# A blockwise inverse laid over 128 partitions instead of 64, even rows in one half and odd rows in the other

## The chip, the cores and the metric

One core of a Trainium2 chip runs the whole program. Its engines are PE (matrix products), DVE (vector), ACT (scalar functions), POOL (a second vector engine) and SP (here it issues every DMA). The metric is the device time of one execution in microseconds.

## The reference, cut to what matters

The program is one encoder layer: a normalised projection, an attention branch, and an RWKV-7 branch with 8 heads of 64 channels in two directions. The RWKV state follows this step, over 2048 and 512 tokens:

```python
def rwkv7_step(S, inp):
    r_t, w_t, k_t, v_t, kk_t, kka_t = inp
    s_kk = jnp.einsum('zbhvk,zbhk->zbhv', S, kk_t)
    S = S * w_t[..., None, :] - s_kk[..., :, None] * kka_t[..., None, :] + v_t[..., :, None] * k_t[..., None, :]
    return S, jnp.einsum('zbhvk,zbhk->zbhv', S, r_t)
```

The kernel computes it in chunks of 64 tokens. Within a chunk, the corrections `s_kk` of 64 tokens depend on one another through a triangular 64 x 64 matrix per head and direction, and the kernel inverts that matrix. It does so in blocks of 32: two triangular 32 x 32 blocks are inverted on DVE, and two small products on PE give the block that joins them.

## The kernel before, in words

The RWKV branch runs in 20 steps (`steps`): four pairs of heads, and in each of them five blocks of 512 tokens (one of them the short sequence) for the two directions. A step has two jobs (one per direction) of 8 chunks x 2 heads = 16 units, so 32 units of 64 x 64.

For each step, `prep` computes decays, the score matrices `SC` (L1177 masks them) and `AT` on PE, ACT, DVE and POOL. `inverse` then inverts, `chain_chunk` carries the state through 8 chunks per direction (its state update is L1289 on DVE, and the next chunk's first product L1259 on PE needs it), and `finish_job` normalises. Beside this, `feed` projects the next heads (L921) to keep PE filled. `do_chain(n)`, `do_inverse(n + 1)` and `do_prep(n + 2)` are written one behind the other, but this is not the order on the engines: every operation goes into a `Plan`, which lists them with a modelled cost and gives each engine a fixed order of its own by the longest remaining path. Each engine then executes its list in order. A tile lives in a named place in SBUF (`memory`, by `lay(tag, size, count)`); an operation that writes a tile whose place another tile used waits for that tile's last reader.

`inverse` in order:

- L1195: 8 DMAs per job bring the 32 x 32 diagonal blocks of `SC` to `ad` in DRAM, so that each of 64 blocks (32 units x 2) is one row of 1024 numbers. L1199 loads `ad` to `M`, 64 partitions x 32 x 32, in the lower half of the tile `X`.
- L1203 to L1206: the norms `ssd` give the scales `rm` and `rs`. L1209 scales the columns of `M`.
- The loop, L1213 and L1214, for i = 1 to 30: column i of `M` times row i, into `tmp`, and the sum into `M`. Both run on DVE on `i` rows and `31 - i` columns, 60 instructions per inverse, each needing the one before.
- L1215 sets the diagonal, L1216 scales the rows, L1217 (ACT) writes the transposed blocks to the upper half of `X`. L1219 stores the transposed blocks to `td[0]`, L1220 the others to `td[1]`.
- For each job: L1226 and L1227 load blocks back into `SC` (8 x 32 KB over the two jobs' units), L1230 loads the transposed first blocks into `bs`, 16 small products (L1233) go to PSUM, L1234 (ACT) copies them negated into `bs`, 16 more (L1237) follow, and L1242 copies the joined block into `SC`. The tile `bs` has one place, so the second job's L1230 waits for the first job's L1237.

## Time and profile before

| | |
|---|---|
| three runs, median (lowest to highest) | 2516.08 us (2509.64 to 2527.17) |
| the profiled execution | 2511.51 us, its span 2509.7 us |
| mean granted TensorE clock of that execution | 0.965 |
| PE, DVE, ACT, POOL busy | 2298.2, 1697.4, 1418.1, 870.8 us |

The span runs from the first to the last instruction of the profiled execution. Busy shares are averages over the span; where a wait matters is read in the stretch of the stage, from the chain of waits and from single rows in order of time. The profiler gives matmuls modelled ends, so PE at 93% of a stretch is not PE at its peak.

### The profile page before, as it was taken

What the parts mean: (1) busy time and instruction counts of PE and PEld (TensorE: products, weight loads), DVE (VectorE), ACT (ScalarE), POOL (GpSimd) and SP (SyncE); (2) the same over time, 40 slices, a digit from 0 to 9 for tenths busy, and PEclk for the clock granted to TensorE, in tenths of its full rate; (3) what the DMA queues carried; (4) which work ended last, traced back from release to release, by engine and by line L of the source; (5) the groups of instructions that cost most, each with busy time, mean ns of one, the idle gap of its engine ahead of it and who ended that gap; (6) DMA issues with size and microseconds to landing.
All of it is one profiled execution on the core that took longest, in us unless ns stands there. A gap on an engine that the chain in (4) does not pass through costs nothing.

```text
span 2509.7 us, 53916 instructions
## 1 busy us (share of the span) xinstructions
PE 2298.2 (92%) x20106; PEld 1652.1 (66%) x20106; DVE 1697.4 (68%) x4248; ACT 1418.1 (57%) x3264; POOL 870.8 (35%) x1059
## 2 busy tenths in 40 slices
PE   6999998987989998989999998999999899999996
PEld 5988997775654654656566665655665677767674
DVE  8874575165754566776887786777777886786445
ACT  7632343365665664667665667666667745554431
POOL 2472564001212154344444443444434533220100
PEclk9999999998999999999999999999999899999998
DMA  7343213367765765454544545655444565554546
GB/s 272 135 145 118 84 60 103 100 186 206 213 190 154 204 201 160 124 156 116 149 137 143 142 131 139 175 146 161 112 136 123 160 190 173 148 156 139 161 159 245
DMA packets 323639, 386.19 MB, mean 154 GB/s; under 512 B 132401, under 2 KB 197809, under 8 KB 321201
## 3 DMA queue, kind: packets, MB, share of 16 engines
q1 hardware_dynamic: 323376, 382.74, 51.9%
q8 instruction: 159, 2.61, 0.4%
q14 instruction: 104, 0.84, 0.1%
HBM read 261.36 MB, written 121.27 MB: 152 GB/s over the span
## 4 chain that ended last, share of the span: by engine, by line
PE 58%; DVE 15%; DMA 14%; ACT 8%; issue 4%; SPq 1%; POOL 1%; DVEq 0%; ACTq 0%; POOLq 0%
PE b L819 15%; PE b L921 11%; PE b L1393 6%; PE b L1175 5%; DVE sbuf L1213 3%; DVE sbuf L1214 3%; DVE sbuf L1289 3%; PE b L1259 3%; PE b L1269 2%; PE b L1262 2%; DMA sbuf<-vad 2%; PE b L1273 2%; PE b L1023 2%; DMA sbuf<-td 1%; DMA sbuf<-xd 1%
## 5 line engine op out<-in xcount | busy, mean ns | idle before, releaser
L921 PE MATMUL b<-sbuf 128*128 128x512 f16 x2040 | 562.6, 387 | 14.6 <-DMA sbuf<-xd 9.4
L819 PE MATMUL b<-sbuf 128*128 128x256 f16 x3840 | 458.5, 276 | 14.6 <-ACT sbuf L839 8.8
L819 PEld LDWEIGHTS <-sbuf 128*128 128x128 f16 x3840 | 374.9, 99 | 64.8 <-issue 12.5
L1393 PE MATMUL b<-sbuf 128*128 128x512 f32 x960 | 287.5, 428 | 20.6 <-DVE sbuf L1402 12.8
L921 PEld LDWEIGHTS <-sbuf 128*128 128x128 f16 x2040 | 177.9, 99 | 179.2 <-issue 22.8
L1289 DVE SCALAR_TENSOR_TENSOR sbuf<-b,sbuf 64x64 f32<-64x64 f32 x568 | 160.2, 282 | 163.9 <-ACT sbuf L1294 97.6
L1213 DVE TENSOR_TENSOR sbuf<-sbuf 64x30 f32<-64x30 f32 (+2 forms) x600 | 252.0, 420 | 11.2
L1214 DVE TENSOR_TENSOR sbuf<-sbuf 64x30 f32<-64x30 f32 (+2 forms) x600 | 247.9, 413 | 11.9
L1393 PEld LDWEIGHTS b<-sbuf 128*128 128x128 f32 x960 | 175.9, 196 | 66.6 <-DVE sbuf L1402 15.5
L1175 PE MATMUL b<-sbuf 128*128 128x128 f32 x1280 | 178.4, 288 | 2.8 <-DVE sbuf L1177 1.2
L1259 PE MATMUL b<-sbuf 128*128 128x128 f32 x608 | 140.8, 315 | 43.7 <-DVE sbuf L1289 25.6
L1175 PEld LDWEIGHTS b<-sbuf 128*128 128x128 f32 x1280 | 163.9, 200 | 16.4 <-issue 4.9
L1259 PEld LDWEIGHTS b<-sbuf 128*128 128x128 f32 x608 | 96.9, 194 | 111.3 <-DVE sbuf L1289 25.3
L1017 DVE CUSTOM_DVE_ANT_0 sbuf<-b,sbuf 128x384 f32<-128x384 f32 (+2 forms) x160 | 90.3, 580 | 113.0 <-PE b L1014 28.4
L1281 ACT ACTIVATE sbuf<-sbuf 128x128 f32<-128x128 f32 x284 | 113.1, 402 | 94.2 <-PE b L1259 91.7
L1273 PEld LDWEIGHTS b<-sbuf 128*64 128x64 f32 x1280 | 100.1, 137 | 85.0 <-ACT sbuf L1270 46.3
L1273 PE MATMUL b<-sbuf 128*64 128x64 f32 x1280 | 143.3, 235 | 13.8 <-ACT sbuf L1270 12.9
L1244 POOL MEMSET sbuf<- 64x512 f32 x80 | 41.1, 518 | 328.0 <-PE b L1277 197.4
L1277 PE MATMUL b<-sbuf 128*64 128x64 f32 x1280 | 152.4, 233 | 0.0
L1269 PE MATMUL b<-sbuf 128*64 128x64 f32 x1280 | 140.3, 235 | 10.0 <-ACT sbuf L1266 9.5
L1269 PEld LDWEIGHTS b<-sbuf 128*64 128x64 f32 x1280 | 100.2, 139 | 74.5 <-ACT sbuf L1266 42.5
L1294 ACT COPY sbuf<-b 64x128 f32<-64x128 f32 x320 | 83.6, 263 | 110.6 <-PE b L1277 57.5
(205 smaller groups left out, 4860.3 us busy)
## 6 DMA issues: line engine op xcount, KB each, us to landing
sbuf<-xd SPq DMA_DIRECT2D x60, 512.0 KB
sbuf<-zrk SPq DMA_DIRECT2D x80, 256.0 KB
sbuf<-zl SPq DMA_DIRECT2D x80, 256.0 KB
sbuf<-in_b_mid_dram SPq DMA_DIRECT2D x32, 512.0 KB
sbuf<-mix SPq DMA_DIRECT2D x28, 448.0 KB
sbuf<-in_x_dram SPq DMA_DIRECT2D x20, 512.0 KB
...
```

The source lines that it names most:

```text
L819: T.matmul(pa, xx[b][:, k, j * 128:(j + 1) * 128], wt[:, k], start=n == 0, stop=n == 23)
L921: T.matmul(pa, W[wt][:, k], xx[k], start=n == 0, stop=n == 23)
L1175: T.matmul(pa[:, u * 128:(u + 1) * 128], both(A[:, u]), z[:, u], start=True, stop=True)
L1213: V.tensor_tensor(out=prod, in0=bc(M[:, 0:i, i:i + 1], i, n), in1=bc(M[:, i:i + 1, i + 1:32], i, n), op=ALU.mult)
L1214: V.tensor_tensor(out=M[:, 0:i, i + 1:32], in0=M[:, 0:i, i + 1:32], in1=prod, op=ALU.add)
L1259: T.matmul(pz[:, 0:128], QR[:, c % 4].rearrange("p a s -> p (a s)"), S0, start=True, stop=False)
L1269: T.matmul(pu[0:64, l0:l0 + 64], SC[:, c % 4, h, 0:64], zs[:, l0:l0 + 64], start=True, stop=True)
L1273: T.matmul(pz[64:128, l0:l0 + 64], SC[:, c % 4, h, 64:128], UV[:, c % 4, l0:l0 + 64], start=S0 is None, stop=S0 is None or h == 1)
L1277: T.matmul(pu[l0:l0 + 64, 128:192], AT[:, c % 4, l0:l0 + 64], UV[:, c % 4, l0:l0 + 64], start=True, stop=True)
L1281: S.activation(out=S0, in_=S0, func=AF.Copy, scale=gt[:, gcol:gcol + 1])
L1289: V.scalar_tensor_tensor(out=S1[l, q], in0=src, scalar=by, in1=S0[l, q], op0=ALU.mult, op1=ALU.add)
L1393: T.matmul(pa, m, w, start=j == 0, stop=j == len(todo) - 1)
```

## The change

The 64 blocks now use 128 partitions. Partition u of the lower half holds the even rows of block u, partition 64 + u the odd rows, 16 rows of 32 each, in a tile `M` of its own. Since each step of the loop multiplies by row i of the block as it was loaded, both halves also get a whole copy of the block, `L` (in the place of `X`), which the loop reads and does not write. A step then runs over (i + 1)//2 rows instead of i.

`ad` is loaded by four DMAs, two whole (for `L`) and two with every second row (for `M`). The scales are prepared on 64 partitions as before, and three ACT copies spread them. The column scaling becomes two products. The transposing copy writes 512 numbers per partition into the front of `L`, with the rows in the order even, odd; the stores go to `tx` (transposed) and `tm` (two DMAs of every second row). `bs` is loaded by two DMAs per job, one per half, and the copy L1249 undoes the order of the columns. `tmp` has no place of its own any more: it is allocated in the one place of `bs`, and `M` takes the place where `tmp` was.

```diff
--- before.py
+++ after.py
@@ -579,7 +579,7 @@
     at = lay(at, *[(t, 32, 2) for t in ("wpam", "wpgs", "wsam", "wsgs", "sums")], ("m", 32, 4))
     end = lay(at, *[(t, 32, 2) for t in ("ss", "rsrx", "rstx", "waam", "wags", "hs")], ("wam", 32, 3),
               *[(t, 32, 1) for t in ("gm", "g8", "rsrg", "rstg")], *[(t, 64, 2) for t in ("ssq", "rsrn", "rstn")])
-    end = max(end, lay(at, ("rs", 256, 1), ("gt", 32, 6),
+    end = max(end, lay(at, ("rs", 384, 1), ("gt", 32, 6),
                        *[(t, 32, 2) for t in ("mean", "var", "rsrf", "rstf")]))
     K = end
     X = K + 40 * KB
@@ -606,7 +606,7 @@
     lay(A, ("lw0", 2 * KB, 1), ("lw1", 2 * KB, 1), ("uph0", KB, 1), ("upl0", KB, 1), ("uph1", KB, 1), ("upl1", KB, 1),
         ("rt", 2 * KB, 2), ("kt", 2 * KB, 2), ("smt", 2080, 1), ("s2", 2080, 1), ("Em", 2080, 1), ("E", 2080, 1),
         ("tha", 2 * KB, 1), ("AK", 2 * KB, 2), ("mkt", KB, 1), ("st", 512, 2), ("rkb", 512, 2),
-        ("QR", 2 * KB, 5), ("bs", 2 * KB, 1), ("tmp", KB, 1), ("zs0", 512, 2), ("zs1", 512, 2))
+        ("QR", 2 * KB, 5), ("bs", 2 * KB, 1), ("M", 2 * KB, 1), ("zs0", 512, 2), ("zs1", 512, 2))
     lay(A + 50 * KB, ("wrh", 2 * KB, 2), ("wrl", 2 * KB, 2), ("AT", 2 * KB, 1), ("QR", 2 * KB, 1))
     lay(end, ("fy", 2 * KB, 1))
     lay(X, ("xx", 4 * KB, 4), ("wrh", 2 * KB, 2), ("wrl", 2 * KB, 2), ("UV", 2 * KB, 6), ("yt", 2 * KB, 3),
@@ -1193,45 +1193,61 @@
                 for k in range(2):
                     l0 = 32 * k
                     D.dma_start(dst[k][:, 8 * i:8 * i + 8], units(SC[l0:l0 + 32])[:, :, l0:l0 + 32])
-        X = tile([128, 32, 32], F32, tag="X", name="X")
-
-        M, X = X[0:64], X[64:128]
-        D.dma_start(M.rearrange("p s t -> p (s t)"), ad)
-        rs = tile([64, 2, 32], F32, tag="rs", name="rs")
-        rm, rs = rs[:, 0], rs[:, 1]
+
+
+        L = tile([128, 32, 32], F32, tag="X", name="L")
+        M = tile([128, 16, 32], F32, tag="M", name="M")
+        rows = lambda ap: ap.rearrange("u (a q t) -> q u a t", q=2, t=32)
+        half = (slice(0, 64), slice(64, 128))
+        for q, l in enumerate(half):
+            D.dma_start(L[l].rearrange("p s t -> p (s t)"), ad)
+            D.dma_start(M[l], rows(ad)[q])
+        rs = tile([128, 3, 32], F32, tag="rs", name="rs")
         for d, J in enumerate(jobs):
-            D.dma_start(rm[32 * d:32 * d + 32], ssd[p][J["b"]][d].rearrange("c h (k t) -> (c h k) t", t=32))
-        V.tensor_scalar(out=rm, in0=rm, scalar1=1e-24, scalar2=2.0, op0=ALU.max, op1=ALU.mult)
-        V.reciprocal(rs, rm)
-        V.tensor_scalar(out=rm, in0=rs, scalar1=-1.0, scalar2=None, op0=ALU.mult)
-        tmp = tile([64, 256], F32, tag="tmp", name="tmp")
-        bc = lambda ap, n, m: ap.to_broadcast([64, n, m])
-        V.tensor_tensor(out=M, in0=M, in1=bc(rm[:, None, :], 32, 32), op=ALU.mult)
+            D.dma_start(rs[32 * d:32 * d + 32, 0], ssd[p][J["b"]][d].rearrange("c h (k t) -> (c h k) t", t=32))
+        V.tensor_scalar(out=rs[0:64, 0], in0=rs[0:64, 0], scalar1=1e-24, scalar2=2.0, op0=ALU.max, op1=ALU.mult)
+        V.reciprocal(rs[0:64, 1], rs[0:64, 0])
+        V.tensor_scalar(out=rs[0:64, 0], in0=rs[0:64, 1], scalar1=-1.0, scalar2=None, op0=ALU.mult)
+        S.copy(out=rs[64:128, 0], in_=rs[0:64, 0])
+        for q, l in enumerate(half):
+            S.copy(out=rs[l, 2, 0:16], in_=rs[0:64, 1, q::2])
+        rm, rs = rs[:, 0], rs[:, 2, 0:16]
+        tmp = tile([128, 256], F32, tag="bs", name="tmp")
+        bc = lambda ap, n, m: ap.to_broadcast([128, n, m])
+        V.tensor_tensor(out=M, in0=M, in1=bc(rm[:, None, :], 16, 32), op=ALU.mult)
+        V.tensor_tensor(out=L, in0=L, in1=bc(rm[:, None, :], 32, 32), op=ALU.mult)
         for i in range(1, 31):
-            n = 31 - i
-            prod = tmp[:, 0:n * i].rearrange("p (s t) -> p s t", t=n)
-            V.tensor_tensor(out=prod, in0=bc(M[:, 0:i, i:i + 1], i, n), in1=bc(M[:, i:i + 1, i + 1:32], i, n), op=ALU.mult)
-            V.tensor_tensor(out=M[:, 0:i, i + 1:32], in0=M[:, 0:i, i + 1:32], in1=prod, op=ALU.add)
-        G.memset(M.rearrange("p s t -> p (s t)")[:, 0:1024:33], 1.0)
-        V.tensor_tensor(out=M, in0=M, in1=bc(rs[:, :, None], 32, 32), op=ALU.mult)
-        S.copy(out=X.rearrange("p t s -> p s t"), in_=M)
-        td = dr.tile([2, 64, 1024], F32, tag="td", name="td", bufs=2)
-        D.dma_start(td[0], X.rearrange("p s t -> p (s t)"))
-        D.dma_start(td[1], M.rearrange("p s t -> p (s t)"))
+
+            n, r = 31 - i, (i + 1) // 2
+            prod = tmp[:, 0:n * r].rearrange("p (s t) -> p s t", t=n)
+            V.tensor_tensor(out=prod, in0=bc(M[:, 0:r, i:i + 1], r, n), in1=bc(L[:, i:i + 1, i + 1:32], r, n), op=ALU.mult)
+            V.tensor_tensor(out=M[:, 0:r, i + 1:32], in0=M[:, 0:r, i + 1:32], in1=prod, op=ALU.add)
+        for q, l in enumerate(half):
+            G.memset(M[l].rearrange("p s t -> p (s t)")[:, q:512:34], 1.0)
+        V.tensor_tensor(out=M, in0=M, in1=bc(rs[:, :, None], 16, 32), op=ALU.mult)
+        X = L[:].rearrange("p s t -> p (s t)")[:, 0:512]
+        S.copy(out=X.rearrange("p (t a) -> p a t", a=16), in_=M)
+        tm = dr.tile([64, 1024], F32, tag="tm", name="tm", bufs=2)
+        tx = dr.tile([128, 512], F32, tag="tx", name="tx", bufs=2)
+        D.dma_start(tx, X)
+        for q, l in enumerate(half):
+            D.dma_start(rows(tm)[q], M[l])
         for d, J in enumerate(jobs):
-            t_ = td[0, 32 * d:32 * d + 32].rearrange("(u k) (s t) -> k s u t", k=2, t=32)
-            tt = td[1, 32 * d:32 * d + 32].rearrange("(u k) (s t) -> k s u t", k=2, t=32)
+            tt = tm[32 * d:32 * d + 32].rearrange("(u k) (s t) -> k s u t", k=2, t=32)
             SU = {i: units(SC[:]) for i, SC in J["SC"].items()}
             for i, t in SU.items():
                 D.dma_start(t[0:32, :, 0:32], tt[0][:, 8 * i:8 * i + 8])
                 D.dma_start(t[32:64, :, 32:64], tt[1][:, 8 * i:8 * i + 8])
             bs = tile([64, 16, 32], F32, tag="bs", name="bs")
             t11 = bs[0:32]
-            D.dma_start(t11, t_[0])
+            for q in range(2):
+                D.dma_start(t11[:, :, 16 * q:16 * q + 16],
+                            tx[64 * q + 32 * d:64 * q + 32 * d + 32].rearrange("(u k) (t a) -> k t u a", k=2, a=16)[0])
             pb = bank("inv")
             for u in range(16):
                 T.matmul(pb[32:64, 32 * u:32 * u + 32], SU[u // 8][0:32, u % 8, 32:64], t11[:, u], start=True, stop=True)
-            S.activation(out=bs[32:64].rearrange("p u t -> p (u t)"), in_=pb[32:64], func=AF.Copy, scale=-1.0)
+            S.activation(out=bs[32:64].rearrange("p u (a q) -> p u a q", q=2),
+                         in_=pb[32:64].rearrange("p (u q a) -> p u a q", q=2, a=16), func=AF.Copy, scale=-1.0)
             pb = bank("inv")
             for u in range(16):
                 T.matmul(pb[0:32, 32 * u:32 * u + 32], bs[32:64, u], SU[u // 8][32:64, u % 8, 32:64],
```

On DVE, this is the place where the eleventh inverse's loop begins, before the change. L1289 is the chain's state update, L691 to L693 and L1154 belong to `finish_job` and `prep`, L1209 scales `M`, and L1213 and L1214 are the loop's first pair.

```order
L1289 SCALAR_TENSOR_TENSOR sbuf<-b_18324,sbuf 64x64 x2
L692 TENSOR_TENSOR sbuf<-sbuf 128x8
L693 SCALAR_TENSOR_TENSOR sbuf<-sbuf 128x8
L691 SCALAR_TENSOR_TENSOR sbuf<-sbuf 128x8
L692 TENSOR_TENSOR sbuf<-sbuf 128x8
L1209 TENSOR_TENSOR sbuf<-sbuf 64x1024
L1154 SCALAR_TENSOR_TENSOR sbuf<-sbuf 128x4x64
L1213 TENSOR_TENSOR sbuf<-sbuf 64x30
L1154 SCALAR_TENSOR_TENSOR sbuf<-sbuf 128x4x64
L1214 TENSOR_TENSOR sbuf<-sbuf 64x30
```

After the change, the same place of the same inverse (L1217 scales `M`, L1223 and L1224 are the loop's first pair, and L1305 is the chain's state update, L1289 before):

```order
L1217 TENSOR_TENSOR sbuf<-sbuf 128x512
L1305 SCALAR_TENSOR_TENSOR sbuf<-b_18520,sbuf 64x64 x2
L692 TENSOR_TENSOR sbuf<-sbuf 128x8
L1154 SCALAR_TENSOR_TENSOR sbuf<-sbuf 128x4x64
L693 SCALAR_TENSOR_TENSOR sbuf<-sbuf 128x8
L1154 SCALAR_TENSOR_TENSOR sbuf<-sbuf 128x4x64
L1305 SCALAR_TENSOR_TENSOR sbuf<-b_18658,sbuf 64x64 x2
L1223 TENSOR_TENSOR sbuf<-sbuf 128x30
L1224 TENSOR_TENSOR sbuf<-sbuf 128x30
L1223 TENSOR_TENSOR sbuf<-sbuf 128x29
```

The loop's first pair has moved back: between the tenth inverse's closing product and it stand 42 instructions now and 25 before, among them 13 of the chain's updates where there were 5. Between the tenth loop's first and last instruction stand 30 others now and 43 before; over all twenty loops, 762 now and 950 before. In 15 of the twenty inverses the first L1223 carries a wait on PE.

On SP, at the same inverse, this is the return of the tenth inverse's blocks before the change (L1226, L1227 and L1230 load from `td`, L1199 loads the eleventh's blocks, L965, L1119 and L1245 are other stages):

```order
L1227 DMA sbuf<-td 32x8x32
L1230 DMA sbuf<-td 32x16x32
L1199 DMA sbuf<-ad 64x1024
L1227 DMA sbuf<-td 32x8x32
L1226 DMA sbuf<-td 32x8x32
L1227 DMA sbuf<-td 32x8x32 x2
L1226 DMA sbuf<-td 32x8x32
L965 DMA zrk_3_18163<-sbuf 128x512
L1119 DMA sbuf<-zl_8430 128x512
```

The second job's L1230 stands 15 rows behind the first. After the change (L1239 and L1240 load from `tm`, L1244 from `tx` into `bs`, L1203 and L1204 the eleventh's blocks):

```order
L1244 DMA sbuf<-tx 32x16x16 x2
L1240 DMA sbuf<-tm 32x8x32 x2
L1195 DMA ad<-sbuf 32x8x32 x2
L1240 DMA sbuf<-tm 32x8x32 x2
L1239 DMA sbuf<-tm 32x8x32 x2
L1203 DMA sbuf<-ad 64x1024 x2
L1204 DMA sbuf<-ad 64x16x32 x2
L1119 DMA sbuf<-zl_8430 128x512
L1244 DMA sbuf<-tx 32x16x16 x2
L1239 DMA sbuf<-tm 32x8x32
```

All loads of the eleventh's blocks now stand between the first job's pair L1244 and the second's, and the second pair has moved up: it stands eight rows behind the first.

## Rows read from the trace of the kernel before

**Rows 1.** Page, part 1: engine, busy us (share of the span), instructions

```profile
PE 2298.2 (92%) x20106; PEld 1652.1 (66%) x20106; DVE 1697.4 (68%) x4248; ACT 1418.1 (57%) x3264; POOL 870.8 (35%) x1059
```

**Rows 2.** Stretch 930 to 2320: length, busy by engine, granted clock, DMA share, GB/s

```profile
930.00:2320.00 1390.00, 1293.91 (x11432) 877.02 (x11431) 1060.50 (x2576) 872.87 (x2079) 550.89 (x752) 0.97 0.52 146
```

**Rows 3.** Chain that ended last, 930 to 2320, shares by line

```profile
by line: PE b L921 12.6%; PE b L1175 7.8%; DVE sbuf L1213 5.3%; PE b L1393 5.2%; DVE sbuf L1214 5.1%; issue 4.5%; DVE sbuf L1289 4.5%; PE b L1259 4.1%; PE b L1269 3.4%; PE b L1262 3.4%; PE b L1273 2.7%; DMA sbuf<-td 2.3%; DMA sbuf<-xd 2.2%;
```

**Rows 4.** Page, part 5, the loop: shapes, count | busy, mean ns | idle before

```profile
L1213 DVE TENSOR_TENSOR sbuf<-sbuf 64x30 f32<-64x30 f32 (+2 forms) x600 | 252.0, 420 | 11.2
L1214 DVE TENSOR_TENSOR sbuf<-sbuf 64x30 f32<-64x30 f32 (+2 forms) x600 | 247.9, 413 | 11.9
```

**Rows 5.** Single lines: count, ns min/median/max, first and last start

```profile
L1213 DVE TENSOR_TENSOR sbuf<-sbuf x600: 170/370/1390, 932.5 to 2314.4; 64x30 f32<-64x30 f32 x10, 64x130 f32<-64x130 f32 x10, 64x198 f32<-64x198 f32 x10, 64x234 f32<-64x234 f32 x10
L1209 DVE TENSOR_TENSOR sbuf<-sbuf x20: 1208/1218/1698, 930.8 to 2281.6; 64x1024 f32<-64x1024 f32 x20
L1217 ACT COPY sbuf<-sbuf x20: 1909/1974/2119, 985.7 to 2316.2; 64x1024 f32<-64x1024 f32 x20
L1234 ACT ACTIVATE sbuf<-b x40: 589/589/592, 996.7 to 2336.5; 32x512 f32<-32x512 f32 x40
```

**Rows 6.** Timelines of DVE, POOL: start, us, line, shapes [idle before]

```profile
1669.12 0.18 DVE L1213 TENSOR_TENSOR sbuf<-sbuf 64x30 f32<-64x30 f32 x1
...
1698.35 0.40 DVE L1213 TENSOR_TENSOR sbuf<-sbuf 64x240 f32<-64x240 f32 x1
...
1578.87 1.27 POOL L1316 TENSOR_TENSOR sbuf<-sbuf 128x512 f32<-128x512 f32 x1 [0.45 <-ACT sbuf L1294]
1579.17 2.05 DVE L1216 TENSOR_TENSOR sbuf<-sbuf 64x1024 f32<-64x1024 f32 x1
```

**Rows 7.** DVE by shape, whole span: busy us, mean ns | idle before

```profile
L1209 DVE TENSOR_TENSOR sbuf<-sbuf 64x1024 f32<-64x1024 f32 x20 | 26.5, 1325 | 42.2 <-DMA sbuf<-ad 42.1
L848 DVE TENSOR_TENSOR sbuf<-sbuf 128x1024 f32<-128x1024 f32 x20 | 25.5, 1273 | 0.7
```

**Rows 8.** Waits, 930 to 2320: who waited for what, us, times, longest

```profile
DVE sbuf L1209 <- DMA sbuf<-ad: 42.1, 17, 5.0
PE b L1259 <- DVE sbuf L1289: 24.0, 53, 1.3
```

**Rows 9.** Timelines of DVE and PE from the tenth to the eleventh inverse

```profile
1526.47 0.35 DVE L1213 TENSOR_TENSOR sbuf<-sbuf 64x30 f32<-64x30 f32 x1
...
1593.08 0.17 DVE L1213 TENSOR_TENSOR sbuf<-sbuf 64x30 f32<-64x30 f32 x1
...
1604.38 1.19 PE L1237 MATMUL b<-sbuf 32*32 32x32 f32 x32
```

**Rows 10.** Timeline of SP's DMA issues at the same place

```profile
1586.56 0.44 SPq L1230 DMA_DIRECT2D sbuf<-td  x1
1587.09 0.47 SPq L1199 DMA_DIRECT2D sbuf<-ad  x1
...
1595.54 0.43 SPq L1230 DMA_DIRECT2D sbuf<-td  x1
```

**Rows 11.** ACT by shape, 1300 to 2000

```profile
L1172 ACT COPY sbuf<-sbuf 64x512 f32<-64x512 f32 x78 | 48.0, 616 | 18.1 <-PE b L1175 11.7 <-POOL sbuf L1163 2.2 <-POOL sbuf L1160 1.9
L1294 ACT COPY sbuf<-b 64x128 f32<-64x128 f32 x159 | 41.6, 263 | 44.0 <-PE b L1277 19.2 <-DVE sbuf L1289 17.1 <-PE b L1262 4.1
```

**Rows 12.** DMA, 1176.5 to 1178.5: packets, MB; the queue's share of 16 engines

```profile
DMA packets 1546, 0.20 MB, mean 100 GB/s; under 512 B 1540, under 2 KB 1540, under 8 KB 1546
q1 hardware_dynamic: 1546, 0.20, 60.6%
```

**Rows 13.** Longest pieces of the chain: start, us; L1217 alone, first and last of nine

```profile
1107.12 1.95 ACT sbuf L1217
...
2160.40 2.08 ACT sbuf L1217
```

## The prediction

> **What bounds the kernel now.** I read the busy shares first. PE is busy 92% of the span, DVE 68%, ACT 57%, POOL 35% [rows 1]. The change touches one stage only, the twenty calls of `inverse`, which run from 930 to 2320 us, so I read that stretch next: of its 1390 us PE is busy 1293.9, DVE 1060.5, ACT 872.9, and the 16 DMA engines 0.52 [rows 2]. PE is therefore the fullest engine and only 96 us of the stretch are left without a matmul; no relief elsewhere can give back more than that. The view to weigh a DVE change by is the chain of waits of the same stretch: the two lines of the inverse's loop, L1213 and L1214, hold 5.3% and 5.1% of it, 144.6 us, and loads from `td` 2.3%, 32 us [rows 3]. Their busy time is 252.0 + 247.9 = 499.9 us in 1200 instructions, 25.0 us per inverse [rows 4]. So 29% of the loop's busy time sets the end and 71% lies beside PE's work.
>
> Then I followed one inverse into the next, the tenth into the eleventh. The tenth's first product starts at 1526.47, its closing product L1216 at 1579.17 [rows 6, 9]. The eleventh's first product starts at 1593.08, while the tenth's last group of small matmuls (L1237) runs until 1604.38 + 1.19 = 1605.57 [rows 9]. The inverses thus overlap by 12.5 us: one iterates on DVE while the other's blocks still come back through DRAM, PE and ACT.
>
> **The change part by part.**
>
> *The loop.* Its 60 instructions stay; each covers half the rows. Undisturbed, 30 elements took 0.18 us and 240 took 0.40 [rows 6]: 1.05 ns per element and 0.149 us fixed. Before, each of the two lines streams the sum of i(31-i) = 4960 elements per partition; after, the sum of (31-i) times (i+1)//2 = 2600. An inverse saves 2 x 2360 x 1.05 ns = 4.95 us; undisturbed it goes from 8.9 + 10.4 = 19.3 to 14.4. That twice the partitions cost nothing is read from 1024 elements on 64 partitions (1325 ns) and on 128 (1273) [rows 7]. The measured 25.0 is 5.7 over the undisturbed 19.3, with single products up to 1390 ns [rows 4, 5]. Do these 5.7 shrink too? One row shows what they are: POOL ran L1316 from 1578.87 to 1580.14, and L1216, begun at 1579.17, took 2.05 us [rows 6], which is the rest of POOL's instruction plus about the 1.1 to 1.2 us of its own. The delay is the remainder of a POOL instruction and not a share of the DVE one, so I let all 5.7 stand: 25.0 becomes 20.05, minus 19.8%. (The Trainium skill, "SBUF — State Buffer", section "Who interferes with whom", says that a DVE instruction with two SBUF inputs and a GpSimd instruction that reads SBUF exclude each other for a whole instruction, with no sharing. By that rule, as by the row, the loss per inverse stays at 5.7; were bandwidth shared instead, the saving would be 25.0 x 4.95 / 19.3 = 6.4 us and the term below 37 us instead of 28.6.) On the chain: 144.6 x 0.198 = **-28.6 us**.
>
> *Closing.* L1216 goes from 1024 to 512 elements, -0.54 us. The transposing copy L1217 takes 1.97 us [rows 5]; half as many elements at its own rate is 0.98 (between 0.62, what 512 plain elements took on ACT [rows 11], and 1.97 if only partitions were added). Among the longest pieces of the chain the copy stands whole nine times, from 1107 to 2160 us [rows 13]. So 9 x (0.54 + 0.98) = **-13.7 us**.
>
> *The return.* The t11 block is loaded by two DMAs of 512 pieces of 64 bytes for one of 512 pieces of 128. One more issue is 0.44 us [rows 10]. Pieces: in two microseconds that held almost only small ones, 1546 took 60.6% of 16 engines, 12.5 ns each [rows 12]; 512 more are 0.4 us over 16 engines. The two t11 loads of an inverse are in series (one `bs` slot): +1.7 us. L1234 takes 0.59 us [rows 5] and now reads and writes with strides; bounds are no loss and a doubling (L1217's 1.93 ns an element against 1.2 for a plain 512), and I take +0.3, twice. Together +2.3 us per inverse, on the chain in the same nine: **+20.7 us**.
>
> *The loads.* `ad` is read by four DMAs instead of one (3 x 0.47 us of SP [rows 10]), 2048 of their pieces 128 bytes; `rs` passes through three small ACT copies (0.26 us each by the nearest row [rows 11]); L1209 becomes two products of 0.68 and 1.22 us. Today DVE waits 42.1 us for that load, 17 times [rows 8], so it would cost: about 3 us of loading, 0.8 of copies and 0.7 of product. I cost it at **nothing** because of the next part: the loop cannot begin earlier anyway. Without that cover it is 20 x 4.5 = 90 us on DVE's queue, of which the loop's 29% is 26 on the chain.
>
> *The new wait.* `tmp` now lies in the slot of `bs`, so the loop's first product must wait until the previous inverse's last L1237 has read `bs`. In the order, 15 of the 20 first products carry a wait on PE. At the handover that moves the loop from 1593.08 to 1605.57 or later, 12.5 us. Behind that product on DVE's in-order queue stand the chain's L1289, for which PE waits (24.0 us in the stretch [rows 8]). The order answers by putting other work ahead of it: 42 instructions instead of 25 between closing product and first product at this handover, and 762 instead of 950 others inside the twenty loops. Is there room? A cycle is (2281.6 - 930.8)/19 = 71.1 us [rows 5]. The tenth inverse's loop lasted 52.7 us with 43 others inside. One that is not the loop's takes (1060.5 - 499.9)/(2576 - 1200) = 0.41 us [rows 2, 4], so 25.0 + 17.6 were work and 10.1 gaps. After, with 30 inside: 20.05 + 12.3 + 10.1 = 42.5. The return lasted 1605.57 - 1579.17 = 26.4 and becomes 26.4 + 0.8 = 27.2. In series 69.7 us, which is under 71.1: I take **0**, with 1.4 us of room.
>
> *Off the path.* 5184 more pieces per inverse (2048 loading, 1984 + 64 storing, 64 for the second copy of L, 1024 for t11) at 12.5 ns are 4.1 us of 16 engines, 81 us in all: 0.52 becomes 0.58. (The Trainium skill, "DMA: Bandwidth & Descriptors", section "Specifications", speaks against such pieces: under 512 bytes an engine reads, modifies and writes. The rows agree that they are poor, about 10 GB/s an engine, but hold too few stores to show a doubling. By that rule, taken as a doubling, the 2048 pieces stored into `tm` cost 1.6 us more per inverse; that store runs beside the copy L1229, so the sum stays.)
>
> **Sum.** -28.6 - 13.7 + 20.7 = -21.6 us. The profiled execution took 2511.5 us (span 2509.7), 4.6 under the median of the three runs; 2511.5 - 21.6 = 2489.9, so I say **2490 us**.
>
> **The rivals.**
>
> *PE takes it all back.* PE is at 93%; where DVE comes sooner, another PE row may stand first. For it: PE's matmuls hold most of the chain. Against it: 96 us without a matmul. Result within 8 us of 2511.
>
> *More than the chain shows.* With 99 us less on DVE the L1289 rows queue less, and half of PE's 96 idle us close: 2511.5 - 48 = 2463. For it: DVE carries 42.5 - 10.1 = 32.4 us in a loop window instead of 42.6. Against it: those L1289 waits are partly for ACT, which hardly changes.
>
> *The new wait becomes the loop that sets the pace (slower).* Place: L1223 behind the last L1253 of the inverse before. It decides from the point where loop and return together pass 71.1 us, 1.4 us away. What could use that up: on SP the second pair of t11 loads now stands eight rows behind the first (before, fifteen), so SP halts there until the first job's L1253; before, L1230 was issued at 1586.56 and 1595.54 [rows 10], 9 us apart, with useful loads between. If 3 us per cycle are lost so, 1.6 remain over the room: 19 x 1.6 = 30 us, and nothing of the gain is left: 2542.
>
> That the wider products don't run faster per row is excluded by [rows 7].
>
> **How the numbers follow.** Forecast (gain of 5 to 50 us): 0.45. PE takes it back: 0.20. More than the chain shows: 0.14. The new wait sets the pace: 0.21. One per cent, 25 us, is about what a measurement of this kernel can tell from no change. Half of the forecast's cases lie beyond 25 us, as do all of the third's: faster 0.36. Of the last, three quarters lie beyond +25: slower 0.16. Same: 0.48. The range runs from inside the third case to the last case's price, 2445 to 2542; the forecast's own is 2462 to 2506.
>
> **What would show it.** DVE's loop lines at about 400 us (from 499.9), means near 335 ns: right. If under 370, the POOL delays shrank too. L1217's successor near 0.98 us, L1234's at 0.6 to 1.2. DVE waits of the first L1223 for PE: short ones mean room; several us in most handovers, with PE below 93% in the stretch, mean that the rival holds and the time is above 2511. A DMA share over 0.62 would say that the pieces cost more than 12.5 ns. The forecast is wrong if the loop lines fall as said and the stretch does not shorten.

## The result, and the profile after

The changed kernel takes **2547.11 us** (median of 4; 2544.39 to 2559.95) against 2513.76 us for the kernel before on the same chip (4; 2509.64 to 2527.17). The ratio is **1.0161** (95%: 1.0128 to 1.0194). The two medians alone give 1.0133, 33 us; 1.61% would be 40 us, and the interval holds both. The forecast was 2490 us, with 2445 to 2542 as its range: the time lies 57 us above the forecast and 5 above the range, on the other side of no change.

The profiled execution after has a span of 2543.3 us at a granted clock of 0.954; before it was 2509.7 at 0.965. Its page, the engines first (busy us, share of the span, instructions), then the DMA packets, then the loop's two lines (count | busy us, mean ns of one | idle before):

```profile
PE 2316.7 (91%) x20106; PEld 1664.7 (65%) x20106; DVE 1609.2 (63%) x4268; ACT 1403.2 (55%) x3324; POOL 853.2 (34%) x1079
...
DMA packets 429241, 396.71 MB, mean 156 GB/s; under 512 B 236720, under 2 KB 302128, under 8 KB 426800
...
L1223 DVE TENSOR_TENSOR sbuf<-sbuf 128x30 f32<-128x30 f32 (+2 forms) x600 | 200.1, 334 | 18.1 <-PE b L1253 5.8
L1224 DVE TENSOR_TENSOR sbuf<-sbuf 128x30 f32<-128x30 f32 (+2 forms) x600 | 192.2, 320 | 12.3
```

DVE lost 88 us of work [rows 1] and the loop 107.6: 499.9 us [rows 4] became 392.3. What the change is for, it does. And yet PE is busy 18 us longer with the same 20106 matmuls.

The chain that ended last, 930 to 2350 us, shares by line:

```profile
by line: PE b L921 9.7%; PE b L1409 6.3%; PE b L1175 5.9%; issue 4.9%; DVE sbuf L1223 4.1%; DVE sbuf L1305 3.9%; DVE sbuf L1224 3.2%; PE b L1275 3.2%; PE b L1285 3.0%; PE b L1278 2.9%; PE b L1289 2.3%; PE b L1248 1.9%; PE b L1253 1.9%; ACT 
```

Against [rows 3] the loop's share falls from 10.4% to 7.3%, from 144.6 to 103.7 us. So 41 us did leave the chain, and something else filled the place.

Now the stretch in which all the loss lies, 920 to 2600 us (length, busy time of PE, weight loads, DVE, ACT and POOL, then granted clock, DMA share, GB/s), before and after. The stretch runs past the end of the shorter span, so idle PE time is span less 920 less busy time:

```profile
920.00:2600.00 1680.00, 1466.63 (x12548) 996.30 (x12546) 1155.05 (x2792) 935.59 (x2243) 572.15 (x775) 0.97 0.49 144
```

```profile
920.00:2600.00 1680.00, 1487.44 (x12566) 1010.55 (x12564) 1068.36 (x2816) 923.58 (x2305) 556.12 (x795) 0.95 0.55 150
```

Before, 1589.7 us were left, 1466.6 of them busy: 123.1 idle. After, 1623.3 and 1487.4: 135.9 idle. Of the 33.6 us by which the profiled span grew, 12.8 are idle PE time and **20.8 are more busy time for the same matmuls**, in a stretch with a granted clock of 0.95 instead of 0.97 (means over time spent at 2.4 and at 1.2 GHz). The mean clock does not settle the busy time by itself: **own_tmp**, a run below, has nearly the idle time (2525.0 - 920 - 1469.6 = 135.4 us) and the clock (0.956) of after, and its PE is busy only 2.9 us longer than before. So how much of the 20.8 the clock makes stays open. The stretch of own_tmp:

```profile
920.00:2600.00 1680.00, 1469.56 (x12535) 1012.77 (x12533) 1086.19 (x2809) 919.15 (x2298) 565.42 (x792) 0.95 0.54 150
```

Over many runs, clock and time do go together. Over the 86 executions of the kernel before that stand beside the runs below (2491.64 us at 0.972 to 2523.96 at 0.963), a fitted line gives 17 us per 0.01 of clock. The 0.011 between the two profiled executions are worth 19 us by it. That says what goes with what, and not which causes which. The next rows show one place in which the clock falls behind idle time.

After, at 1206.92 us, the chain waits 6.21 us for a load of `xd`, the operand of L921, from its issue to its landing. First the chain's piece (start, us, what), then five stretches around it in the columns above, then the packets under way while PE waits:

```profile
1206.92 6.21 DMA sbuf<-xd
```

```profile
1186.00:1189.90 3.90, 3.63 (x37) 2.02 (x35) 2.21 (x5) 2.94 (x8) 1.97 (x5) 1.00 0.51 114
1189.90:1197.20 7.30, 7.26 (x53) 5.06 (x51) 5.69 (x13) 6.67 (x17) 0.00 (x1) 1.00 0.82 203
1197.20:1206.90 9.70, 7.99 (x111) 6.16 (x111) 3.16 (x6) 8.11 (x19) 6.73 (x12) 1.00 0.84 161
1206.90:1213.20 6.30, 4.80 (x73) 3.85 (x73) 2.83 (x7) 2.89 (x8) 1.49 (x2) 0.94 0.94 262
1213.20:1223.00 9.80, 9.66 (x83) 5.56 (x82) 5.07 (x16) 3.78 (x11) 2.78 (x6) 0.87 0.83 283
```

```profile
DMA packets 2455, 1.65 MB, mean 262 GB/s; under 512 B 1795, under 2 KB 2027, under 8 KB 2454
## 3 DMA queue, kind: packets, MB, share of 16 engines
q1 hardware_dynamic: 2454, 1.64, 93.8%
```

The DMA engines are full (0.94), 1795 of 2455 packets are under 512 bytes, PE drops from 7.26 of 7.30 us to 7.99 of 9.70 and then 4.80 of 6.30, and the clock from 1.00 to 0.87 in the stretch after. The averages of the stage (0.57 DMA, 0.95 clock) show none of this. It is one place; how much such places cost in all is what the runs with whole pieces below measure.

### The profile page after: what moved, and what is told of

Its sections match the earlier page's. It is cut to its first block, busy times and chain, and to the rows that moved or that the text cites. A ratio compares the mean times of both kernels' runs of the same rounds, so it can differ in the third digit from the quotient of the medians.

```text
span 2543.3 us, 54276 instructions
## 1 busy us (share of the span) xinstructions
PE 2316.7 (91%) x20106; PEld 1664.7 (65%) x20106; DVE 1609.2 (63%) x4268; ACT 1403.2 (55%) x3324; POOL 853.2 (34%) x1079
## 4 chain that ended last, share of the span: by engine, by line
PE 27%; DVE 11%; ACT 5%; DMA 5%; issue 3%; SPq 2%; POOL 1%; DVEq 0%; ACTq 0%; POOLq 0%
PE b L1409 7%; PE b L921 5%; PE b L1175 3%; DVE sbuf L1305 2%; DVE sbuf L1223 2%; PE b L1275 2%; PE b L1285 2%; DVE sbuf L1224 2%; PE b L1278 2%; PE b L1289 1%; PE b L1248 1%; ACT sbuf L1310 1%; PE b L1253 1%; DMA sbuf<-tx 1%; DMA sbuf<-xd 1%
## 5 line engine op out<-in xcount | busy, mean ns | idle before, releaser
L921 PE MATMUL b<-sbuf 128*128 128x512 f16 x2040 | 571.0, 391 | 20.9 <-DMA sbuf<-xd 16.8
L921 PEld LDWEIGHTS <-sbuf 128*128 128x128 f16 x2040 | 179.5, 99 | 193.1 <-issue 37.6
L1305 DVE SCALAR_TENSOR_TENSOR sbuf<-b,sbuf 64x64 f32<-64x64 f32 x568 | 160.5, 283 | 175.9 <-ACT sbuf L1310 86.2
L1223 DVE TENSOR_TENSOR sbuf<-sbuf 128x30 f32<-128x30 f32 (+2 forms) x600 | 200.1, 334 | 18.1 <-PE b L1253 5.8
L1224 DVE TENSOR_TENSOR sbuf<-sbuf 128x30 f32<-128x30 f32 (+2 forms) x600 | 192.2, 320 | 12.3
L1293 PE MATMUL b<-sbuf 128*64 128x64 f32 x1280 | 157.9, 236 | 0.0
L1289 PEld LDWEIGHTS b<-sbuf 128*64 128x64 f32 x1280 | 101.7, 140 | 85.1 <-ACT sbuf L1286 48.5
L1289 PE MATMUL b<-sbuf 128*64 128x64 f32 x1280 | 144.5, 237 | 11.1 <-ACT sbuf L1286 10.1
L1177 DVE TENSOR_TENSOR sbuf<-b,sbuf 128x512 f32<-128x512 f32 x160 | 109.9, 689 | 62.5 <-PE b L1175 38.2
L1278 PE MATMUL b<-sbuf 128*64 128x64 f32 x1280 | 146.0, 237 | 1.4 <-DMA sbuf<-tm 0.8
L1285 PE MATMUL b<-sbuf 128*64 128x64 f32 x1280 | 140.7, 236 | 6.9 <-ACT sbuf L1282 6.1
```

Source lines behind the costliest of these rows:

```text
L921: T.matmul(pa, W[wt][:, k], xx[k], start=n == 0, stop=n == 23)
L1223: V.tensor_tensor(out=prod, in0=bc(M[:, 0:r, i:i + 1], r, n), in1=bc(L[:, i:i + 1, i + 1:32], r, n), op=ALU.mult)
L1224: V.tensor_tensor(out=M[:, 0:r, i + 1:32], in0=M[:, 0:r, i + 1:32], in1=prod, op=ALU.add)
L1278: T.matmul(pz[0:64, l0:l0 + 64], SC[:, c % 4, h, 0:64], UV[:, c % 4, l0:l0 + 64], start=S0 is None, stop=S0 is None or h == 1)
L1285: T.matmul(pu[0:64, l0:l0 + 64], SC[:, c % 4, h, 0:64], zs[:, l0:l0 + 64], start=True, stop=True)
L1289: T.matmul(pz[64:128, l0:l0 + 64], SC[:, c % 4, h, 64:128], UV[:, c % 4, l0:l0 + 64], start=S0 is None, stop=S0 is None or h == 1)
```

## Experiments: the relief by itself

**before_half** is the kernel before with the loop over (i + 1)//2 rows on its 64 partitions: the shorter instructions alone.

```diff
-            n = 31 - i
-            prod = tmp[:, 0:n * i].rearrange("p (s t) -> p s t", t=n)
+            n, r = 31 - i, (i + 1) // 2
+            prod = tmp[:, 0:n * r].rearrange("p (s t) -> p s t", t=n)
```

> The kernel before with the loop over (i + 1)//2 rows instead of i, still on 64 partitions: the products and sums of the other rows are left out. It has the relief of DVE (about 99 us busy) and nothing else of the change: no second load, no copies, no new wait, no other return. The prediction's term by the chain of waits: 28.6 us faster, 2480 to 2490. The rival that PE takes it all back: within 8 us of before. The rival that the chain of waits undervalues it: below 2470.

Measured: 0.9992 (0.9973 to 1.0012). The loop is as short as it should be (400.3 us busy) and nothing is gained. But the plan models each instruction's cost, so a shorter loop also gives a new order on every engine. **half_fixed** leaves the instructions of before_half and charges the plan the old cost, so that the order on every engine is that of before:

```diff
-        op = Op(len(self.ops), eng, call, args, kw, self.cost(eng, call, out, reads, kw), self.boost)
+        op = Op(len(self.ops), eng, call, args, kw, self.cost(eng, call, out, reads, kw) if self.full is None else 0.068 + self.full * 0.00104, self.boost)
...
+            plan.full = n * i
```

> As before_half (loop over (i + 1)//2 rows on 64 partitions; the other rows' products are left out), but the planner still counts the full rows, so that every engine's order is that of the kernel before, instruction by instruction. It shows what shorter loop instructions are worth with no reshuffle at all. Chain of waits: 28.6 us faster, ratio 0.985 to 0.992. PE takes it back: ratio 0.997 or more. If it is clearly faster while before_half was not, the reshuffle of before_half hid a gain.

Measured: **0.9897** (0.9863 to 0.9932), so 26 us faster at the same order (about 9 either way). Its loop lines on the page, and the chain's shares by engine over its whole span:

```profile
L1214 DVE TENSOR_TENSOR sbuf<-sbuf 64x30 f32<-64x30 f32 (+2 forms) x600 | 200.2, 334 | 11.6
L1213 DVE TENSOR_TENSOR sbuf<-sbuf 64x30 f32<-64x30 f32 (+2 forms) x600 | 195.3, 326 | 11.2
```

```profile
PE 66%; DMA 13%; ACT 8%; DVE 7%; issue 3%; SPq 1%; POOL 1%; DVEq 0%; ACTq 0%; POOLq 0%
```

The loop is busy 395.5 us, 104 less than before and close to the changed kernel's 392.3. DVE holds 7% of the chain, before it held 15% (both over the whole span). Between before_half and half_fixed only the order differs: it is worth 0.95% (0.4 either way), nearly the whole relief.

**before_plan** and **before_p66** ask how much an order is worth by chance. Both are the kernel before with nothing in the program changed but one modelled constant of the plan:

```diff
-        return (0.068 + n * (0.00104 if two or psum else 0.00052) + (0.061 if n > 1 else 0) * pointers)
+        return (0.070 + n * (0.00104 if two or psum else 0.00052) + (0.061 if n > 1 else 0) * pointers)
```

> The kernel before, computing the same with the same instructions, except that the planner's fixed cost of a DVE operation is 0.070 us instead of 0.068, so that some instructions change places. It measures what a reshuffled order is worth by itself. Theory W and theory R both expect it within 8 us of before; if it moves by more than 20 us, then no difference of that size between two of these kernels can be put down to the parts of the change without more runs.

> The kernel before with the planner's fixed DVE cost at 0.066: a third draw of its order (0.068 is the reference, 0.070 gave 0.9912). It says how far orders alone scatter: if within 0.4% of the reference, 0.070 was a lucky one and the reference is typical; if as fast as 0.070, the reference itself is an unlucky one, and the change's true cost is larger than 1.6%.

Measured: 0.9912 (0.9893 to 0.9932) with 0.070, and 0.9982 (0.9958 to 1.0006) with 0.066. before_plan moved by 20 us where at most 8 were expected. The same work thus lies within 0.9% by the order alone, over three draws. A difference of half a per cent between two kernels with different orders says nothing about their parts; an edit has to be tested in more than one draw, or at a fixed order. before_plan, at **2489.75 us**, is also the fastest kernel here that leaves nothing out; it beats both kernels.

**before_half_p70** is before_half with 0.070, the shorter loop in the second draw.

> before_half (half of the loop's rows left out, nothing else changed) with the planner's fixed DVE cost at 0.070, a second draw of its order. Its partner is before_plan (0.9912). If a reshuffle for shorter loop instructions loses the relief as a rule: 0.988 to 0.994, no better than before_plan. If before_half drew a bad order: 0.978 to 0.985, the 1.03% of half_fixed on top of before_plan.

Measured: 0.9892 (0.985 to 0.9934), 0.2% under before_plan (0.5 either way). So in both draws (0.1% and 0.2%) a plan that knows of the shorter loop gives back most of the 1.03% that it is worth at the fixed order of the first. Why the plan does so, I did not find out. The timelines show a part of it: in before_half the loop's window shrank from 53.1 to 43.8 us, but the return, from the closing product to the last small matmul, grew from 29.4 to 35.7 (means over the second to the sixteenth inverse); at the old order, in half_fixed, they are 51.6 and 29.3.

## Experiments: the wait of `tmp` for `bs`

**own_tmp** is the changed kernel with 512 bytes for `tmp` alone, so that the loop doesn't wait for the return.

```diff
-        ("QR", 2 * KB, 5), ("bs", 2 * KB, 1), ("M", 2 * KB, 1), ("zs0", 512, 2), ("zs1", 512, 2))
+        ("QR", 2 * KB, 5), ("bs", 2 * KB, 1), ("M", 2 * KB, 1), ("tmp", 512, 1), ("zs0", 512, 2), ("zs1", 512, 2))
...
-        tmp = tile([128, 256], F32, tag="bs", name="tmp")
+        tmp = tile([128, 128], F32, tag="tmp", name="tmp")
```

> The changed kernel with one thing undone: tmp gets a place of its own again (512 bytes per partition, which is all that 128 numbers need), so the loop's first product no longer waits for the last small matmul of the inverse before. Theory W (this wait sets the pace: loop and return stand in series): the loop starts 10 to 15 us before the previous return's end again, and the time falls from 2547 us to 2480 to 2515. Theory R (the wait is planned around and harmless; the longer return, the eight extra DMAs per inverse and the 103,680 extra pieces cost the time): it stays within 10 us of 2547. In between (2520 to 2537), both have a part.

Measured: 1.0056 (1.002 to 1.0092). That is 1.05% less than the changed kernel (0.5 either way), and 2525 us lies where the expectation gives both theories a part. Since the two kernels also have different orders, the scatter of the orders is in these 1.05%.

**before_shared** puts the same wait into the kernel before.

```diff
-        tmp = tile([64, 256], F32, tag="tmp", name="tmp")
+        tmp = tile([64, 256], F32, tag="bs", name="tmp")
```

> The kernel before with one part of the change alone: tmp is allocated in the place of bs. Loads, loop, return and stores are untouched. Theory W: the return of 29.4 us and a loop of about 53 us, part of which moves into the gap, come into series against a cycle of 69 to 71 us: slower than before by 30 to 100 us (2545 to 2615). Theory R: within 10 us of before.

Measured: 1.0275 (1.0252 to 1.0299). Its stretch from 920 to 2600 us, and what its loop's first line waited for (us, times):

```profile
920.00:2600.00 1680.00, 1510.32 (x12549) 1024.49 (x12547) 1155.46 (x2791) 930.59 (x2244) 586.41 (x775) 0.94 0.49 144
```

```profile
  PE b L1237: 22.4, 9
```

With the long loop the two in series don't fit, as the prediction's own sum says (52.7 + 26.4 = 79 us over a cycle of 71). The clock falls to 0.94 and PE is busy 43.7 us longer than before, at the old DMA share of 0.49. So here the clock falls, and PE is busy longer, with no small pieces added. The 2.75% lie well outside the 0.9% by which orders alone scatter.

**after_p70** and **own_tmp_p70** are the changed kernel and own_tmp with the plan's constant at 0.070, a second draw of the order.

> The changed kernel with the planner's fixed DVE cost at 0.070 instead of 0.068, as in before_plan: a second draw of the order for the change. If the changed kernel's loss of 1.6% is the change's and not one order's: it stays 1.0 to 2.5% above before (0.068) and 2 to 3% above before_plan. If the loss was mostly that order's luck: within 0.5% of before or faster.

> own_tmp (the change without the shared place) with 0.070: a second pair for the wait. Theory W: 0.8 to 1.5% faster than after_p70 (the first pair gave 1.0%). Theory R, with the first pair explained by the order: within 0.4% of after_p70.

Measured: 1.007 (1.0039 to 1.0102) and 1.0037 (1.0012 to 1.0061). The kernel with the shared place is 0.33% slower in this draw (0.4 either way, so not clear of nothing), where it was 1.05% slower in the first. By the expectation on record, under 0.4% speaks for the order as the explanation of the first pair. What the place itself costs the changed kernel is therefore not settled. In this draw the changed kernel stands 0.7% above before and 1.6% above before_plan, its partner; that is the loss of the first draw again.

**after_nowait** keeps the changed kernel's order (all but eight memsets on POOL) and gives `tmp` a place of its own behind the plan's back: the wait is gone, the order that it forced is not.

```diff
-        tmp = tile([128, 256], F32, tag="bs", name="tmp")
+        tmp = tile([128, 256], F32, tag="bs", name="tmp"); tmp.make = tile([128, 128], F32, tag="tmp", name="tmp2").real
```

> The changed kernel with tmp in a place of its own, while the planner still believes that it lies in the place of bs: the order of PE, DVE, ACT and SP is that of the changed kernel instruction by instruction (POOL's differs in eight places, all memsets before the first inverse), only the hardware's wait of the loop for the last L1253 is gone. Theory W1 (the engines stand and wait there): most of the 15 to 27 us between the changed kernel and own_tmp comes back, ratio to before 1.004 to 1.010. Theory W2 (nobody waits much there, DVE's waits for it came to 5.8 us in all; what costs is the order that the wait forces on the planner, with the loop pushed behind the return): within 5 us of the changed kernel, ratio 1.013 to 1.018.

Measured: 1.0164 (1.0128 to 1.02), the time of the changed kernel. DVE's standing at the semaphore (5.8 us in all, on the page line of L1223 above) costs nothing that these runs can tell (0.5% either way). What after and own_tmp differ by is the **order**. Its stretch from 920 to 2600 us is nearly that of after:

```profile
920.00:2600.00 1680.00, 1485.39 (x12547) 1010.61 (x12545) 1076.38 (x2811) 921.12 (x2300) 555.38 (x795) 0.95 0.54 150
```

What that order looks like, in the changed kernel's timelines of DVE and PE (start, us, line, shapes): a closing product, the last group of small matmuls of its return, the next loop's first product and its closing product.

```profile
1545.80 0.69 DVE L1227 TENSOR_TENSOR sbuf<-sbuf 128x512 f32<-128x512 f32 x1
```

```profile
1571.96 0.31 PE L1253 MATMUL b<-sbuf 32*32 32x32 f32 x4
```

```profile
1572.30 0.17 DVE L1223 TENSOR_TENSOR sbuf<-sbuf 128x30 f32<-128x30 f32 x1
...
1608.50 0.67 DVE L1227 TENSOR_TENSOR sbuf<-sbuf 128x512 f32<-128x512 f32 x1
```

The next loop starts 0.03 us after the last matmul of the return. I went through all nineteen handovers so: in 16 the loop starts between 3.3 us before and 0.3 after the end of that last group, in three 1.8 to 8.2 us later. Before, the loop started 4.8 to 37.8 us *before* the return's end in all nineteen, as in [rows 9]. Loop and return now stand in series, and DVE seldom waits, since other work has been put ahead of the loop. Whether that work is missed later, no run shows.

## Experiments: the small pieces

These runs keep the order of the kernel that they start from (the plan is charged the 128-byte pieces) and change only the size of the pieces, 64 rows of 2 KB instead of 1024 of 128 bytes per DMA (256 pieces per inverse over the four DMAs, not the 128 that the first expectation says). They leave out the dealing of even and odd rows. SP needs about as long to issue them: a load of `M`, L1204, takes 610 ns in after and 596 in after_whole (medians). **own_tmp_whole** does it for the two loads of `M` and the two stores to `tm`, **own_tmp_load** and **own_tmp_store** for one of them each, and **after_whole** for both in the changed kernel itself.

```diff
-            D.dma_start(M[l], rows(ad)[q])
+            plan.as_run = 128; D.dma_start(M[l], whole(ad)[q]); plan.as_run = None
...
-            D.dma_start(rows(tm)[q], M[l])
+            plan.as_run = 128; D.dma_start(whole(tm)[q], M[l]); plan.as_run = None
```

> own_tmp with the 4096 pieces of 128 bytes per inverse (loads of M, stores to tm) replaced by 128 pieces of 2 KB: each partition takes half a block as it lies, so the rows in M are not the even and odd ones and the output is not the reference's. Number of DMAs and the order of every engine are own_tmp's. If the small pieces cost nothing on the path (the prediction: they lie beside other work): within 4 us of own_tmp, ratio to before 1.002 to 1.009. If they are what eats the relief of DVE: 15 us or more faster than own_tmp, ratio below 1.000.

> own_tmp, order unchanged, with only the stores to tm made of 2 KB pieces (64 per DMA instead of 1024; the rows stored are not the right ones, so the output is not the reference's). Both kinds together gave 0.92% (1.0056 to 0.9964). If the stores cause it: ratio 0.995 to 0.999. If the loads do: 1.003 to 1.008. If each has half: 1.000 to 1.003.

> own_tmp, order unchanged, with only the loads of M made of 2 KB pieces (each partition loads half a block as it lies, so the output is not the reference's). If the loads cause the 0.92%: ratio 0.995 to 0.999. If the stores do: 1.003 to 1.008.

> The changed kernel itself, order unchanged, with the loads of M and the stores to tm in 2 KB pieces (wrong rows, as in own_tmp_whole). If the small pieces cost the changed kernel what they cost own_tmp (0.92%): ratio to before 1.004 to 1.010. If the wait's order hides them (the load lies under the wait there, as predicted): 1.012 to 1.017.

| run | pieces of 2 KB | ratio to before (95%) |
|---|---|---|
| own_tmp | none | 1.0056 (1.002 to 1.0092) |
| own_tmp_store | stores | 1.0008 (0.9984 to 1.0033) |
| own_tmp_load | loads | 0.9986 (0.9963 to 1.0009) |
| own_tmp_whole | both | 0.9964 (0.994 to 0.9988) |
| after | none | 1.0161 (1.0128 to 1.0194) |
| after_whole | both | 1.003 (1.0005 to 1.0055) |

At a fixed order the pieces cost own_tmp 0.92% and the changed kernel **1.31%** of the 1.61% that it loses (each 0.4 either way); its median falls by 30 us, from 2547.11 to 2517.12. Where PE stood for them is seen in the line of L921 on the pages of after and of after_whole (count | busy us, mean ns | idle before):

```profile
L921 PE MATMUL b<-sbuf 128*128 128x512 f16 x2040 | 571.0, 391 | 20.9 <-DMA sbuf<-xd 16.8
```

```profile
L921 PE MATMUL b<-sbuf 128*128 128x512 f16 x2040 | 565.7, 388 | 13.3 <-DMA sbuf<-xd 8.9
```

Before, L921 waited 9.4 us for `xd`: with whole pieces the change's surplus is gone. In own_tmp it waits 8.2 us and in own_tmp_whole 9.8, so there the gain comes by another way. The stretch from 920 to 2380 us of own_tmp and of own_tmp_whole, and one wait of each (who waited for what: us, times, longest):

```profile
920.00:2380.00 1460.00, 1351.17 (x11889) 927.53 (x11888) 1015.90 (x2649) 882.39 (x2199) 559.22 (x787) 0.95 0.57 152
```

```profile
DVE sbuf L1208 <- DMA sbuf<-ssd: 30.2, 15, 7.8
```

```profile
920.00:2380.00 1460.00, 1363.04 (x12050) 932.41 (x12048) 1030.33 (x2688) 895.35 (x2231) 567.35 (x795) 0.96 0.54 156
```

```profile
DVE sbuf L1208 <- DMA sbuf<-ssd: 19.5, 8, 7.1
```

With whole pieces 161 more matmuls fit into the same stretch, the DMA share is 0.03 lower, and a small load that is not part of the change, `ssd`, is waited for 19.5 us instead of 30.2. Over the span, that wait is 30.5 us in own_tmp, 30.0 with the loads whole and 22.1 with the stores whole. So the pieces go with later loads of other data, `xd` in the changed kernel and `ssd` in own_tmp; they need not be waited for themselves. How much of the 0.92% the wait for `ssd` makes, no run shows.

The Trainium skill, "DMA: Bandwidth & Descriptors", section "Specifications", says that transfers under 512 bytes are read, modified and written. I read that as a burden on writes, by which the stores should be the dear half. The runs show 0.48% for the stores and 0.70% for the loads, each 0.4 either way: no sign of it, and no proof against it.

**lean** goes the other way and drops the two loads of `M`. It forms `M` from `L` in the column scaling, on DVE, with the real rows:

```diff
-            D.dma_start(M[l], rows(ad)[q])
...
-        V.tensor_tensor(out=M, in0=M, in1=bc(rm[:, None, :], 16, 32), op=ALU.mult)
+        for q, l in enumerate(half):
+            V.tensor_tensor(out=M[l], in0=L[l].rearrange("p (a q) t -> p q a t", q=2)[:, q],
+                            in1=rm[l, None, :].to_broadcast([64, 16, 32]), op=ALU.mult)
```

> own_tmp without the two loads of M: M is formed from L, which both halves have, by the scaling product itself (two products of 512 elements on 64 partitions instead of one on 128, 0.68 us more DVE per inverse). Two DMAs and 2048 pieces fewer per inverse, and the loop can start when the two whole loads have landed. If the longer load, uncovered once the wait is gone (priced at 26 us on the chain in the prediction), is what is left of the loss: 10 us or more faster than own_tmp, at or below before. If not: within an order's scatter of own_tmp, ratio 1.000 to 1.010.

Measured: 1.0069 (1.0036 to 1.0102), no better than own_tmp (1.0056). It has an order of its own and one more DVE instruction per inverse, so by the scatter of the orders it neither bears the 0.70% of the loads out nor speaks against it. I count it as inconclusive.

**lean_store** also stores `M` in one DMA of 2 KB pieces, and pays at the other end: each load from `tm` into `SC` becomes two, into every second partition. **lean_store_p70** is its second draw.

```diff
-        for q, l in enumerate(half):
-            D.dma_start(rows(tm)[q], M[l])
+        D.dma_start(tm, M.rearrange("p s t -> p (s t)"))
...
-                D.dma_start(t[0:32, :, 0:32], tt[0][:, 8 * i:8 * i + 8])
+                for q in range(2):
+                    D.dma_start(t[q:32:2, :, 0:32], tt[q][0][:, 8 * i:8 * i + 8])
```

> lean (M formed from L on the chip, tmp in a place of its own) and in addition one store to tm in 2 KB pieces; the even and odd rows are put apart by the loads instead, 16 per inverse with 16 partitions each instead of 8 with 32 (same number of 128-byte pieces loaded as before the change). Of the change's extra pieces only t11's are left. Nothing of the computation is left out. Small pieces as the main cost (own_tmp_whole: 0.92%): ratio 0.994 to 1.001, against 1.0069 for lean. If the eight more DMAs on SP cost as much as the pieces gave: 1.003 to 1.010.

> lean_store with the planner's fixed DVE cost at 0.070, a second draw of its order. If 0.070 is the better setting for this design too (before 0.0088 better, the change 0.0091, own_tmp 0.0019): 0.985 to 0.996, possibly below before_plan's 0.9912, which is so far the fastest kernel that leaves nothing out. If the scatter is blind: within 0.6% of lean_store on either side.

Measured: 1.0501 (1.0452 to 1.055) and 1.0452 (1.0401 to 1.0504), the worst of all. SP's issue of one of the two loads in lean_store, then in lean (ns min/median/max), and the chain's shares by engine in lean_store:

```profile
L1241 SPq DMA_DIRECT2D sbuf<-tm x160: 555/598/1393, 983.1 to 2434.7; - x160
```

```profile
L1241 SPq DMA_DIRECT2D sbuf<-tm x80: 302/449/1973, 981.4 to 2307.2; - x80
```

```profile
PE 55%; DMA 16%; DVE 13%; ACT 6%; SPq 5%; issue 4%; POOL 1%; DVEq 0%; ACTq 0%; POOLq 0%
```

Not only are there twice as many, each also takes 598 ns to issue instead of 449. Over the two lines that is 320 x 0.598 - 160 x 0.45 = 119 us more on SP's queue. Between the medians of lean_store and lean lie 118 us, between their ratios 4.3%, 108 us. SP holds 5% of lean_store's chain. The sums are close, but the loads may also land later (DMA has 16% of the chain), and no run separates the two. lean_store thus doesn't say what the pieces of the stores cost.

## Why the prediction was wrong, point by point

Two steps failed: a gain read from the chain was taken as if the order stayed, and the small pieces were put off the path at nothing. The sign that the prediction set for itself came true: the loop lines fell as said and the stretch did not shorten.

**The loop's relief: right.** Predicted: loop lines at about 400 us and -28.6 us. Measured: 392.3 us, and 26 us at a fixed order (half_fixed), so neither "PE takes it all back" nor "more than the chain shows" holds for the relief itself. The 5.7 us of POOL delays per inverse, which I let stand, are 392.3 / 20 - 14.4 = 5.2 after. The Trainium skill, "SBUF — State Buffer", section "Who interferes with whom", has the two engines exclude each other for a whole instruction, and the trace agrees: with shared bandwidth each inverse would, by the prediction, have saved 6.4 of its 25.0 us, and the lines would be at 372 us.

**That relief on the chain stays gained: wrong.** The sum took the chain of before and shortened its links as if the order stayed. In a kernel whose order is planned from modelled costs it does not. In both draws the new order gave most of the relief back (before_half, before_half_p70). This step was not named as a step at all, and in the first draw it alone takes away 0.95%.

**The new wait at nothing: right for the wait, wrong for the room, open for the order.** The hardware's wait is indeed nothing (5.8 us; after_nowait). Between the kernels with and without the shared place lie 1.05% and 0.33% in the two draws, and the scatter of the orders is in both. The sum "69.7 us in series, under 71.1" had its two terms in place: the loop's window was put at 42.5 us and is 40.6; the return was put at 27.2 and is 31.4 (means over the second to the sixteenth inverse). The return was read from the one handover in [rows 9], 26.4 us; its mean over the same inverses before was 29.4. Measured, the two make 72.0 us, so the 1.4 us of room were never there. The columns' scaling L1217 starts at these times (count, ns min/median/max, first and last start):

```profile
L1217 DVE TENSOR_TENSOR sbuf<-sbuf x20: 678/687/994, 936.3 to 2314.4; 128x512 f32<-128x512 f32 x20
```

The cycle is (2314.4 - 936.3) / 19 = 72.5 us, where [rows 5] gave 71.1. Nineteen times 1.4 us are 27 of the 33.6 us. But the series alone doesn't make them. In after_whole, at the same order, loop and return stand in series as well (in 16 handovers the loop starts between 4.6 us before and 0.3 after the last group's end, in three 1.3 to 7.2 later), the two take 40.8 and 30.1 us, and L1217 starts from 930.7 to 2283.1 us: a cycle of 71.2, that of before. With the small pieces the return is 1.3 us longer, and in series that goes into every cycle. The rival's mechanism was close, but its price was put on SP's halt, of which the return of 30.1 us, 0.7 over before where +0.8 was priced, shows no sign. Its sign, "short waits mean room", was wrong: the wait had been turned into order.

**The small pieces off the path: wrong, the largest step as measured.** The volume was right: predicted a DMA share of 0.58, measured 0.57 in the stretch of [rows 2]. The price of "off the path" was not nothing but 1.31%, some 30 us, in the changed kernel. The mean share of 0.57 hides places like the one at 1206.92 us, at 0.94, where a load of `xd` comes late.

**The loads at nothing: open.** I let the new wait hide them. L1208 waits 14.9 us for `ssd` after and waited 9.0 before, and L1218 waits 32.6 us for `ad` where L1209 waited 42.1 [rows 8]. With whole pieces after_whole shows 10.1 and 28.6. The two views don't separate the number of the loads from their pieces.

**The return and the closing: sizes off.** The return was to grow by 0.8 us and grew by 2.0, from 29.4 to 31.4 (with whole pieces by 0.7). From the end of the transposing copy to the first small matmul it takes 9.8 us, before 7.6; one pair of t11 loads lies in there, priced at +0.85, so about 1.3 of the 2.2 came from elsewhere. With whole pieces it is still 9.6. The +0.3, twice, for the strides of L1249 isn't there. The closing's two instructions came out near their prices, L1227 at 0.69 us (0.68) and the transposing copy at 1.07 (0.98). What they gave on the chain can't be read: the copy stands whole in it four times, where the sum took nine.

```profile
L1249 ACT ACTIVATE sbuf<-b x40: 588/588/590, 999.1 to 2364.7; 32x512 f32<-32x512 f32 x40
```

```profile
L1229 ACT COPY sbuf<-sbuf x20: 1039/1066/1096, 985.3 to 2341.8; 128x512 f32<-128x512 f32 x20
```

The copy nearly halves, at 2.08 ns an element where [rows 5] gave 1.93; reading PSUM with the columns reordered costs L1249 nothing against [rows 5].

**PE's busy time as constant: wrong.** The sums are in us of the old clock and leave PE's busy time as it was. Of the 33.6 us lost, 20.8 are busy PE time, beside a lower granted clock. That is no fixed rate: after lost 2.6 us for each us of idle time, own_tmp (15.3 us of span for 12.3 of idle) 1.2.

The steps added up, as ratios to before, each step about 0.4% either way. half_fixed, the relief at the old order: 0.9897. To own_tmp_whole: +0.67%, which holds the re-planned order, the extra loads, copies and t11 loads, less the shorter closing; the runs don't divide it. To after_whole, loop and return in series: +0.66%. To after, the pieces: +1.31%. Together 1.0161. The first and the last link are at a fixed order; the middle two also hold the scatter of the orders, up to 0.9% over three draws.
